# Gate and up of every second feed-forward tile as seven block products, on one Trainium2 core

## The chip, the cores and the metric

The kernel runs on one core of one Trainium2 chip. The time is device time in microseconds of one execution. Before the change it was 1366.73 us, the median of 3 runs (1365.81 to 1369.22).

## What is computed

The reference is a model of two layers on 512 tokens of width 1024, all in fp32. The first layer mixes tokens by two kinds of attention and then applies a feed-forward block; the second is a short convolution and a mixture of experts. The change touches the feed-forward block of the first layer alone, with a hidden width of 2816:

```
def swiglu(x, w_gate, w_up, w_down):
    return (jax.nn.silu(x @ w_gate) * (x @ w_up)) @ w_down

x = x + swiglu(rms_norm(x, ev_ffn_norm[i]), ffn_w_gate[i], ffn_w_up[i], ffn_w_down[i])
```

## The kernel before

**Precision.** An fp32 number is carried as two parts of type fp32r, "high" (a rounded copy, made on ScalarE) and "low" (the rest, a subtraction on VectorE); `split` (L517) makes such a pair. `mm3` (L512) makes one product of 128 rows in three matmuls: high times high, high times low, low times high. The sum is kept in PSUM.

**The feed-forward stage.** The hidden width is 22 tiles of 128 features (`NF`, index f). The normed input is held transposed in four buffers, `b0h`, `b0l`, `b1h`, `b1l` (each half of the model width, high and low, all 512 tokens). For one tile, `product_of_next` (L1404) takes one weight piece, runs `product` (L1383: 8 blocks of the model width, three matmuls of 512 columns each, so 24) into one PSUM bank, and releases the piece. It is called for gate and for up. `ff_tile` (L1411) then makes silu(gate) on ScalarE, the product with up on VectorE, and splits the result into hT[f] (ScalarE, then VectorE). `ff_down` (L1418) multiplies up to four finished tiles with the down weights: for each of 4 row blocks of 128 tokens and each half of the output columns it sums over the tiles in PSUM, and VectorE adds the sum into x. Within a row block the tiles are taken in order of f. The order is written out by `ffn_order` (L54): tiles 0 to 3, down for 0 and 1, tiles 4 to 7, down for 2 to 5, tiles 8 to 11, down for 6 to 9, and so on; tiles 20 and 21, down for 18 to 21. Tiles 0 and 1 are done together by `first` (L1387), in two halves of 256 tokens, while the norm of the last tokens is still being made.

**Weights.** `Weights` keeps a list of chunks (DMA loads of 512 KB) and of pieces (up to 128 x 1024 numbers, split into high and low). `pump` (L331) issues the next load when a raw buffer is free (on SyncE's queue), and otherwise the next split when its chunk is loaded and one of the part buffers is free: a copy on ScalarE (L351) and a subtraction on VectorE (L352). In this stage there are 6 raw buffers and 6 part buffers (`weight_room` "wa", L463, and "wb", L1270). `use` takes the next piece; `done` (L369) gives its part buffer back and pumps, so the split of the sixth piece on is written into the queues of ScalarE and VectorE at that place of the program:

```
def done(self, *pieces, splits=99):
    self.part_free += [p.slot for p in pieces]
    self.pump(splits)
```

**Order.** The program is scheduled by hand (`manual_schedule`): each engine works its instructions off in the order in which the code issues them; semaphores between engines are put in by the framework. PSUM is two pools of four banks: "p" (transposes, down products) and "g" (gate and up).

Of the kernel before, what the change touches and what calls it, by code (L numbers as in the profile page):

```python
# [13 lines left out]
F32 = mybir.dt.float32  # L14
F32R = mybir.dt.float32r
I32 = mybir.dt.int32
BF16 = mybir.dt.bfloat16
AF = mybir.ActivationFunctionType
OP = mybir.AluOpType
# [5 lines left out]
T = 512  # L25
D = 1024
NT = T // 128
KD = D // 128
# [6 lines left out]
NF = FF // 128  # L35
# [5 lines left out]
PACE = 2  # L41
GATE_UP_PACE = (1, 3, 2, 2)
NTINY = 8
MIX_ORDER = (1, 3, 0, "latent", "t0", "lq0", "c0", "lkv", "t1", "c1", "c2", "lq1", "k0", 2, "q", "k1")
WHOLE_HEADS = 2
WHOLE_TILES = 8
CW = 2048
PW = 1024
# [129 lines left out]
class Buf:  # L178


    def __init__(self, region, shape, dtype):
        self.region, self.shape, self.dtype = region, shape, dtype
        self.log, self.tile, self.before, self.over = [], None, None, False
        self.last, region.last = region.last, self
# [61 lines left out]
class Plan:  # L246
# [14 lines left out]
    def add(self, engine, n, issue, reads=(), writes=()):  # L261
        fixed, rate = self.RATE[engine]
        op = len(self.ops)
        deps = set()
        for bufs, write in ((reads, False), (writes, True)):
            for b in bufs:
                buf, part = b if isinstance(b, tuple) else (b, None)
                deps |= buf.touch(op, part, write)
        deps.discard(op)
        self.ops.append((engine, fixed + n / rate, issue, deps))  # L270
# [32 lines left out]
class Weights:  # L303
# [22 lines left out]
    def add_part(self, src, offset, row, at, k, n, keep=False):  # L326

        self.pieces.append(Piece(len(self.chunks), 0, k, n, keep))
        self.chunks.append((bass.AP(tensor=src.tensor, offset=src.offset + offset + at, ap=[[row, 128], [1, k * n]]), k * n))

    def pump(self, pieces=99):  # L331

        while True:
            if self.loaded < len(self.chunks) and self.raw_free:
                ap, m = self.chunks[self.loaded]
                pool, tag = slot = self.raw_free.pop(0)
                t = pool.tile([128, PW], F32, name=tag, tag=tag, bufs=1)
                self.nc.sync.dma_start(t[:, :m], ap)
                self.raw[self.loaded] = t, slot
                self.loaded += 1  # L340
            elif (pieces and self.ready < len(self.pieces) and self.pieces[self.ready].chunk in self.raw
                  and self.part_free):
                pieces -= 1
                p = self.pieces[self.ready]
                self.ready += 1
                raw, raw_slot = self.raw[p.chunk]
                pool, tag = p.slot = self.part_free.pop(0)
                p.t = pool.tile([128, 2, PW], F32R, name=tag, tag=tag, bufs=1)
                m = p.k * p.n
                src = raw[:, p.at:p.at + m]  # L350
                self.nc.scalar.copy(p.t[:, 0, :m], src)  # L351
                self.nc.vector.tensor_tensor(p.t[:, 1, :m], src, p.t[:, 0, :m].bitcast(F32), op=OP.subtract)  # L352
                if p.keep:
                    p.raw, p.raw_slot = self.raw.pop(p.chunk)
                else:
                    self.raw_free.append(self.raw.pop(p.chunk)[1])
            else:
                return
# [26 lines left out]

class Piece:
    def __init__(self, chunk, at, k, n, keep):
        self.chunk, self.at, self.k, self.n, self.keep = chunk, at, k, n, keep

    def hi(self, k, cols=slice(None)):  # L390
        return self.t[:, 0, k * self.n:(k + 1) * self.n][:, cols]
# [3 lines left out]

    def whole(self, k):
        return self.raw[:, k * self.n:(k + 1) * self.n]


class Act:  # L400
# [26 lines left out]
def kernel(ctx: ExitStack, tc: tile.TileContext, A, out, stop=None):  # L427
    nc = tc.nc
    PE, DVE, ACT, POOL = nc.tensor, nc.vector, nc.scalar, nc.gpsimd
# [26 lines left out]
    W = Weights(nc)  # L456
# [28 lines left out]
    og = od = 0  # L485
    for do, f in FFN_ORDER:
        if do == "up":
            og = W.add(A["w_gu"], og, (KD, 128), (KD, 128))
        else:
            for _ in range(0, f[1], 2):  # L490
                od = W.add(A["w_down"], od, (1, D), (1, D))
# [17 lines left out]
                off = W.add(A["w_ed"], off, (2, 512), (n - 2, 512), keep=True)  # L509


    def mm3(o, lh, ll, rh, rl, start, stop):  # L512
        PE.matmul(o, lh, rh, start=start, stop=False)  # L513
        PE.matmul(o, lh, rl, start=False, stop=False)  # L514
        PE.matmul(o, ll, rh, start=False, stop=stop)  # L515

    def split(hi, lo, src):  # L517
        ACT.copy(hi, src)  # L518
        DVE.tensor_tensor(lo, src, hi.bitcast(F32), op=OP.subtract)
# [60 lines left out]
    with ExitStack() as l0:  # L580
# [668 lines left out]
        for c in range(2):  # L1249
            ws = [take(), take()]  # L1250
            for i in range(NT):
                p = F2.buf([128, 512])
                s = slice(i * 128, (i + 1) * 128)
                for kb in range(2):
                    def go(p=p, s=s, kb=kb, w=ws[kb][0]):
                        for k in range(2):
                            mm3(p(), oh[0]()[:, 2 * kb + k, s], ol[0]()[:, 2 * kb + k, s], w.hi(k), w.lo(k),
                                kb == 0 and k == 0, kb == 1 and k == 1)
# [128 lines left out]
    def first(n, late, finish):  # L1387

        ws = []
        ps = [psB.tile([128, T], F32, name="pg", tag="g") for _ in range(n)]  # L1390
        for half in range(2):
            for j in range(n):
                if half == 0:
                    ws.append(W.use())
                product(ps[j], ws[j], slice(256 * half, 256 * half + 256))
                if half == 0 and j in late:
                    late[j]()
                if half == 1:
                    W.done(ws[j])
                    if j in finish:  # L1400
                        finish[j](ps)
        return ps

    def product_of_next():  # L1404
        w = W.use()
        p = psB.tile([128, T], F32, name="pg", tag="g")
        product(p, w, everything)
        W.done(w)
        return p

    def ff_tile(f, pg, pu):  # L1411
        sg = work.tile([128, T], F32, name="sg", bufs=2)
        hT[f] = work.tile([128, 2, T], F32R, name="hT", tag="hT", bufs=6)
        ACT.activation(sg, pg, AF.Silu)
        DVE.tensor_tensor(sg, pu, sg, op=OP.mult)
        split(hT[f][:, 0], hT[f][:, 1], sg)

    def ff_down(f0, nf, mid, end):  # L1418
# [18 lines left out]
        for f in range(nf):  # L1437
            del hT[f0 + f]

    nothing = lambda i: None  # L1440
    late = {0: lambda: transpose(2), 1: lambda: transpose(3)}
    for n, (do, f) in enumerate(FFN_ORDER):
        if do == "down":
            if n == len(FFN_ORDER) - 1:
                if stop == 2:
                    ff_down(*f, nothing, dump)
                    return
                xT2 = Act(act, "a")
                norm, transpose = normer(xT2, row_tile, psA, "p")
                ff_down(*f, *handover(norm, transpose))  # L1450
            else:
                ff_down(*f, nothing, nothing)
        elif f == 0:
            first(4, late, {1: lambda ps: ff_tile(0, *ps[:2]), 3: lambda ps: ff_tile(1, *ps[2:])})
        elif f > 1:
            pg = product_of_next()
            ff_tile(f, pg, product_of_next())
    load_gain(3)
    xT = xT2
# [6 lines left out]

    def conv_tile(j, pc, pu, pb):
        z = zs[j % 2]
        ct = work.tile([128, T], F32, name="sg", bufs=2)
        ACT.copy(ct, pc)  # L1470
        DVE.tensor_tensor(z[:, 2:], pu, ct, op=OP.mult)
        y = work.tile([128, T], F32, name="y", bufs=2)
        w = [pp[:, PP_CONV + 3 * j + a:PP_CONV + 3 * j + a + 1] for a in range(3)]
        DVE.tensor_scalar(y, z[:, 2:], w[2], None, op0=OP.mult)
        for a in (1, 0):
            DVE.scalar_tensor_tensor(y, z[:, a:a + T], w[a], y, op0=OP.mult, op1=OP.add)
        DVE.tensor_tensor(y, pb, y, op=OP.mult)
        split(yT.hi(j, everything), yT.lo(j, everything), y)
# [54 lines left out]
    def transpose(i):  # L1533

        hl = split_rows[i] = [work.tile([128, KD, 128], F32R, name="hT", tag="hT", bufs=6) for _ in range(2)]
        for b in range(2):
            pt = psA.tile([128, 4, 128], F32, name="pt", tag="p")
            for j in range(4):
                k = 4 * b + j
                PE.transpose(pt[:, j], xr[i][:, k * 128:(k + 1) * 128], ident)  # L1540
            split(hl[0][:, 4 * b:4 * b + 4], hl[1][:, 4 * b:4 * b + 4], pt)

    def logits(i):
        h, l = split_rows.pop(i)
        p = psB.tile([16, 128], F32, name="plT", tag="g")
        for k in range(KD):
            if k == 0:
                PE.matmul(p, wr[:, k], h[:, k], start=True, stop=False)
            PE.matmul(p[:8], wr[:, k, :8], l[:, k], start=False, stop=False)
            if k:  # L1550
                PE.matmul(p, wr[:, k], h[:, k], start=False, stop=k == KD - 1)
        lT = work.tile([16, 128], F32, name="sg", bufs=2)
        ACT.copy(lT, p)
        return lT

# [477 lines left out]
```

## Time and profile before

| | us |
|---|---|
| median of 3 runs | 1366.73 |
| the profiled execution | 1367.42 |
| its span | 1365.7 |
| TensorE busy | 1332.3 |
| VectorE busy | 844.6 |
| ScalarE busy | 688.8 |

Times in the profile are us from the span's start unless marked ns. PE is TensorE's matmul, PEld its weight load, DVE is VectorE, ACT ScalarE, POOL GpSimd, SP SyncE. PEclk is the granted TensorE clock as a share of 2.4 GHz. Matmuls are pipelined, so their bars overlap: the time between two starts is the pace, not the length of a bar. Names that begin with w, a, b or c and end in p, as `wap`, are part buffers of weights; `wbr` is a raw buffer.

### The profile page before, as it was taken

To read this page: it belongs to the slowest core of one execution; us is meant where nothing else is said; L and a number is where in the kernel's file an instruction comes from. 1 tells how busy PE (TensorE), PEld (TensorE's weight loads), DVE (VectorE), ACT (ScalarE), POOL (GpSimd) and SP (SyncE) were. 2 spreads that over 40 slices of the span, in tenths; PEclk is the share of its full clock that TensorE was granted. 3 is DMA by queue.
4 is the path that set the end of the run, shared out by engine and by line. 5 is a ranking of instruction groups with operands and counts; after the bars stand their busy time and mean duration, and the time that the engine had idled before them with its cause. 6 is when DMAs were issued, how large, how long until landed. Compare 5 with 4: busy or idle time off the path is not lost. (4 is left out here: it accounts for less than half of the span.)

```text
span 1365.7 us, 19159 instructions
## 1 busy us (share of the span) xinstructions
PE 1332.3 (98%) x6956; PEld 1061.4 (78%) x6957; DVE 844.6 (62%) x1365; ACT 688.8 (50%) x1144; POOL 208.2 (15%) x309
## 2 busy tenths in 40 slices
PE   7999899999999999999999999999999999999997
PEld 6866687879888888888898888888877878677774
DVE  4348897956433433434355444588888789786864
ACT  4535887854322222222242222377767678575763
POOL 2257554320000000000000000020111101201001
PEclk9999999999999999999999999999999999999999
DMA  5243101123321313132233222299997989979692
GB/s 191 88 157 113 32 17 47 47 101 124 116 93 63 131 61 133 62 124 75 95 109 108 93 93 78 103 340 321 401 341 258 358 326 399 324 250 338 231 342 53
DMA packets 69175, 229.83 MB, mean 168 GB/s; under 512 B 8768, under 2 KB 10060, under 8 KB 69068
## 3 DMA queue, kind: packets, MB, share of 16 engines
q1 hardware_dynamic: 64332, 217.39, 44.4%
q0 software_dynamic: 3392, 9.48, 2.9%
q10 hardware_dynamic: 1344, 1.58, 0.4%
q8 instruction: 62, 1.02, 0.3%
q14 instruction: 45, 0.37, 0.1%
HBM read 219.47 MB, written 8.94 MB: 167 GB/s over the span
## 5 line engine op out<-in xcount | busy, mean ns | idle before, releaser
L352 DVE TENSOR_TENSOR wbp<-wbr,wbp 128x1024 fp32r<-128x1024 f32 (+2 forms) x91 | 107.3, 1194 | 145.1 <-ACT wbp L351 143.2
L351 ACT CAST wbp<-wbr 128x1024 fp32r<-128x1024 f32 (+2 forms) x91 | 92.1, 1026 | 203.5 <-PE pg L515 109.1
L352 DVE TENSOR_TENSOR wap<-wbr,wap 128x1024 fp32r<-128x1024 f32 (+1 forms) x88 | 103.6, 1192 | 96.2 <-ACT wap L351 95.1
L351 ACT CAST wap<-wbr 128x1024 fp32r<-128x1024 f32 (+1 forms) x88 | 89.5, 1027 | 113.0 <-PE pg L515 73.5
L352 DVE TENSOR_TENSOR wap<-wcr,wap 128x1024 fp32r<-128x1024 f32 (+2 forms) x84 | 90.9, 1114 | 16.5 <-ACT wap L351 10.9
L352 DVE TENSOR_TENSOR wbp<-wcr,wbp 128x1024 fp32r<-128x1024 f32 (+2 forms) x83 | 91.6, 1129 | 12.4 <-ACT wbp L351 10.6
L524 POOL TENSOR_TENSOR rs<-rs,mhalf 128x1 f32<-128x1 f32 x11 | 6.1, 551 | 566.4 <-DVE rs L523 566.4
L351 ACT CAST wap<-wcr 128x1024 fp32r<-128x1024 f32 (+2 forms) x84 | 78.4, 962 | 18.7 <-DMA wcr<-w_eg 9.2
L351 ACT CAST wbp<-wcr 128x1024 fp32r<-128x1024 f32 (+2 forms) x83 | 79.4, 977 | 16.0 <-DMA wcr<-w_eg 6.5
L513 PE MATMUL pg<-wap,xgTh 128*128 128x512 f32 (+1 forms) x168 | 64.1, 382 | 0.7
L513 PE MATMUL pg<-wbp,xgTh 128*128 128x512 f32 (+1 forms) x162 | 61.7, 381 | 1.0
L515 PE MATMUL pg<-wap,xgTl 128*128 128x512 f32 (+1 forms) x168 | 62.5, 372 | 0.0
L514 PE MATMUL pg<-wap,xgTh 128*128 128x512 f32 (+1 forms) x168 | 62.4, 372 | 0.0
L514 PE MATMUL pg<-wbp,xgTh 128*128 128x512 f32 (+1 forms) x162 | 60.3, 372 | 0.0
L515 PE MATMUL pg<-wbp,xgTl 128*128 128x512 f32 (+1 forms) x162 | 60.3, 372 | 0.0
L1434 DVE TENSOR_TENSOR x<-pd,x 128x512 f32<-128x512 f32 x48 | 32.3, 689 | 39.2 <-PE pd L515 39.1
L612 POOL TENSOR_TENSOR s<-s,mhalf 128x4 f32<-128x4 f32 (+4 forms) x37 | 35.3, 963 | 70.2 <-DVE s L611 55.6
L1735 POOL DMA_INDIRECT xg<-xd,idx x15 | 22.9, 1530 | 140.6 <-DVE idx L1694 120.0
L636 DVE TENSOR_TENSOR wap<-r,wap 128x1024 fp32r<-128x1024 f32 (+3 forms) x24 | 26.2, 1091 | 26.5 <-ACT wap L633 26.4
L1897 POOL DMA_INDIRECT out_dram<-y,idx x7 | 14.9, 2128 | 174.5 <-ACT xe L1760 174.5
L513 PE MATMUL pd<-wap,hT 128*128 128x512 f32 x104 | 41.2, 396 | 0.0
L515 PE MATMUL pd<-wap,hT 128*128 128x512 f32 x104 | 41.1, 395 | 0.0
(531 smaller groups left out, 3926.4 us busy)
## 6 DMA issues: line engine op xcount, KB each, us to landing
wcr<-w_ed SPq DMA_DIRECT2D x50, 512.0 KB
wcr<-w_eg SPq DMA_DIRECT2D x45, 512.0 KB
wbr<-w_gu SPq DMA_DIRECT2D x44, 512.0 KB
wcr<-w_eu SPq DMA_DIRECT2D x40, 512.0 KB
wbr<-w_ed SPq DMA_DIRECT2D x30, 512.0 KB
wbr<-w_od_in SPq DMA_DIRECT2D x24, 512.0 KB
wbr<-w_eu SPq DMA_DIRECT2D x24, 512.0 KB
wbr<-w_down SPq DMA_DIRECT2D x22, 512.0 KB
```

Source lines behind the costliest of these rows:

```text
L351: self.nc.scalar.copy(p.t[:, 0, :m], src)
L352: self.nc.vector.tensor_tensor(p.t[:, 1, :m], src, p.t[:, 0, :m].bitcast(F32), op=OP.subtract)
L513: PE.matmul(o, lh, rh, start=start, stop=False)
L514: PE.matmul(o, lh, rl, start=False, stop=False)
L515: PE.matmul(o, ll, rh, start=False, stop=stop)
L524: POOL.tensor_tensor(dst, dst, mhalf[:p, :m], op=OP.pow)
L612: op("POOL", 70 + 78 * n, lambda: POOL.tensor_tensor(rs(), rs(), mhalf[:rs().shape[0], :n], op=OP.pow), (), [buf])
L636: op("DVE", m, lambda: DVE.tensor_tensor(p.t[:, 1, :m], src(), p.t[:, 0, :m].bitcast(F32), op=OP.subtract), [raw], [part])
L1434: DVE.tensor_tensor(x[i][:, cs], ps[c], x[i][:, cs], op=OP.add)
L1735: POOL.indirect_dma_start(out=t, out_offset=None, in_=src, in_offset=rows_of(e, b, n))
L1897: POOL.indirect_dma_start(out=out, out_offset=rows_of(e, 0), in_=y, in_offset=None, compute_op=OP.add)
```

## The change

Every odd tile from 3 to 21 (`SEVEN`, ten tiles) is computed as a product of 2 x 2 blocks: the two column blocks are gate and up, the model width is cut in two halves (the rows of the weights), and the tokens in two halves of 256. Seven products of blocks (each 4 blocks of 128 of the model width, three matmuls of 256 columns) take the place of eight. Sums of weight blocks are made on VectorE when a piece is split (four additions of 128 x 512; four pieces a tile in place of two, the last of them half as long, from the same 1 MB of weights). Sums of activation blocks are made once: POOL puts the high and low parts together again (`unsplit`), and VectorE and ScalarE make and split four sums after the gate product of tile 2 (`right_sums`). Four of the seven products are summed in one PSUM bank `a`, whose value is read between them; `b` and `e` are two halves of a second bank. ScalarE and VectorE collect the four results in `r`.

```
+SEVEN = tuple(range(3, NF, 2))
...
+    def add_products(self, src, offset, scratch):
+        for m in range(2):
+            self.chunks.append((bass.AP(tensor=src.tensor, offset=src.offset + offset + m * PW,
+                                        ap=[[2 * PW, 128], [1, PW]]), PW))
+        self.pieces += Products(self.nc, len(self.chunks) - 2, scratch).pieces
+        return offset + 128 * 2 * PW
...
+                if p.group:
+                    free = p.group.split(p, *(self.raw[p.group.chunk + j][0] for j in range(2)))
+                    if free is not None:
+                        self.raw_free.append(self.raw[free][1])
+                    continue
...
+class Products:
+    def __init__(self, nc, chunk, scratch):
+        self.nc, self.chunk, self.scratch = nc, chunk, scratch
+        self.pieces = [Piece(chunk + 1, 0, k, 128, False) for k in (8, 8, 8, 4)]
+        for p in self.pieces:
+            p.group = self
+
+    def split(self, p, a, b):
+        h, nc, j = PW // 2, self.nc, self.pieces.index(p)
+        add = nc.vector.tensor_tensor
+        if j == 0:
+            s = self.scratch()
+            self.src = [a, s, b, a[:, h:]]
+        src = self.src[j]
+        m = src.shape[1]
+        nc.scalar.copy(p.t[:, 0, :m], src)
+        if j == 0:
+            add(s[:, h:], a[:, :h], b[:, :h], op=OP.subtract)
+            add(b[:, :h], b[:, :h], b[:, h:], op=OP.add)
+            add(s[:, :h], b[:, :h], a[:, :h], op=OP.subtract)
+        add(p.t[:, 1, :m], src, p.t[:, 0, :m].bitcast(F32), op=OP.subtract)
+        if j == 0:
+            add(a[:, h:], a[:, h:], s[:, :h], op=OP.subtract)
+        return {2: self.chunk + 1, 3: self.chunk}.get(j)
...
-                og = W.add(A["w_gu"], og, (KD, 128), (KD, 128))
+            if f in SEVEN:
+                og = W.add_products(A["w_gu"], og, lambda: work.tile([128, PW], F32, name="sums", bufs=1))
+            else:
+                og = W.add(A["w_gu"], og, (KD, 128), (KD, 128))
...
-        sg = work.tile([128, T], F32, name="sg", bufs=2)
+        sg = work.tile([128, T], F32, name="sg", tag="R", bufs=2)
...
+    def unsplit(s):
+        for kb in range(2):
+            w = whole[kb, s] = work.tile([128, 4, T // 2], F32, name="whole", tag="hT", bufs=6)
+            POOL.tensor_tensor(w, xT.h[kb][:, :, tok2[s]].bitcast(F32), xT.l[kb][:, :, tok2[s]].bitcast(F32), op=OP.add)
+
+    def right_sums():
+        t1, t3, t4, t2 = whole[0, 0], whole[0, 1], whole[1, 0], whole[1, 1]
+        for dst, a, b in ((t1, t3, t1), (t3, t2, t3), (t2, t2, t1), (t4, t4, t2)):
+            DVE.tensor_tensor(dst, a, b, op=OP.subtract)
+        for j, t in ((2, t2), (3, t3), (1, t1), (4, t4)):
+            split(sums[j - 1][:, 0], sums[j - 1][:, 1], t)
...
+    def ff_products(f):
+        a, be = (psB.tile([128, 2, T // 2], F32, name="pg", tag="g") for _ in range(2))
+        a, b, e = a[:, 0], be[:, 0], be[:, 1]
+        r = work.tile([128, 3, T // 2], F32, name="R", bufs=2)
+        hT[f] = work.tile([128, 2, T], F32R, name="hT", tag="hT", bufs=6)
+
+        def go(p, w, k0, right, start):
+            for k in range(4):
+                mm3(p, w.hi(k0 + k), w.lo(k0 + k), right.hi(k), right.lo(k), start and k == 0, k == 3, more=not start)
+
+        def add(dst, x, y):
+            DVE.tensor_tensor(dst, x, y, op=OP.add)
+
+        w1 = W.use()
+        go(a, w1, 0, B11, True)
+        ACT.copy(r[:, 0], a)
+        go(b, w1, 4, B21, True)
+        W.done(w1)
+        w2 = W.use()
+        go(a, w2, 0, T2, False)
+        add(r[:, 0], b, r[:, 0])
+        ACT.copy(r[:, 1], a)
+        w3 = W.use()
+        go(e, w3, 0, T1, True)
+        ACT.copy(r[:, 2], e)
+        go(a, w2, 4, T3, False)
+        add(r[:, 2], a, r[:, 2])
+        W.done(w2)
+        w4 = W.use()
+        go(e, w4, 0, B22, False)
+        add(r[:, 1], e, r[:, 1])
+        ACT.activation(r[:, 0:2], r[:, 0:2], AF.Silu)
+        go(a, w3, 4, T4, False)
+        DVE.tensor_tensor(r[:, 0], a, r[:, 0], op=OP.mult)
+        DVE.tensor_tensor(r[:, 1], r[:, 2], r[:, 1], op=OP.mult)
+        two_of = lambda j: hT[f][:, j].rearrange("p (a t) -> p a t", a=2)
+        split(two_of(0), two_of(1), r[:, 0:2])
+        W.done(w4, w3)
...
+    unsplit(0)
+    late = {0: lambda: transpose(2), 1: lambda: transpose(3), 2: lambda: unsplit(1)}
...
+        elif f in SEVEN:
+            ff_products(f)
         elif f > 1:
             pg = product_of_next()
+            if f == 2:
+                right_sums()
             ff_tile(f, pg, product_of_next())
```

The buffers `ct` (convolution) and `lT` (router) also take the tag `R`, and `mm3` hands an argument for a check of open sums through.

## Rows read from the trace of the kernel before

**Rows 1.** The page: span, and busy time of the engines.
```profile
span 1365.7 us, 19159 instructions
PE 1332.3 (98%) x6956; PEld 1061.4 (78%) x6957; DVE 844.6 (62%) x1365; ACT 688.8 (50%) x1144; POOL 208.2 (15%) x309
```

**Rows 2.** Stretch: length; PE, PEld, DVE, ACT, POOL busy; clock, DMA share, GB/s.
```profile
321.00:612.00 291.00, 291.00 (x1361) 240.86 (x1360) 116.84 (x132) 81.97 (x98) 0.55 (x1) 1.00 0.31 103
```

**Rows 3.** Timeline, TensorE, from tile 3 on: start, length, line, out<-in, tile.
```profile
356.48 0.39 PE L513 MATMUL pg<-b0h,wbp 128*128 128x512 f32 x1
...
367.46 0.39 PE L513 MATMUL pd<-wap,hT 128*128 128x512 f32 x1
...
375.40 0.39 PE L514 MATMUL pd<-wap,hT 128*128 128x512 f32 x1
```

**Rows 4.** Timeline, TensorE, the 24 matmuls of 256 columns from 321.12.
```profile
321.12 0.28 PE L513 MATMUL pg<-b0h,wbp 128*128 128x256 f32 x1
...
323.83 0.28 PE L515 MATMUL pg<-b1h,wbp 128*128 128x256 f32 x1
...
321.36 0.19 PEld L513 LDWEIGHTS pg<-b0h,wbp 128*128 128x128 f32 x1
```

**Rows 5.** Timeline, ScalarE, end of tile 2's up product.
```profile
351.23 1.05 ACT L351 CAST wap<-wbr 128x1024 fp32r<-128x1024 f32 x1 [1.93 <-PE pg L515]
356.72 1.05 ACT L351 CAST wbp<-wbr 128x1024 fp32r<-128x1024 f32 x1 [4.44 <-PE pg L515]
357.67 0.59 ACT L1414 ACTIVATE sg<-pg 128x512 f32<-128x512 f32 x1
359.67 0.62 ACT L518 CAST hT<-sg 128x512 fp32r<-128x512 f32 x1 [1.40 <-DVE sg L1415]
```

**Rows 6.** Timeline, VectorE, the same place.
```profile
357.81 1.23 DVE L352 TENSOR_TENSOR wbp<-wbr,wbp 128x1024 fp32r<-128x1024 f32 x1 [4.27 <-ACT wbp L351]
358.95 0.68 DVE L1415 TENSOR_TENSOR sg<-pg,sg 128x512 f32<-128x512 f32 x1
360.32 0.69 DVE L519 TENSOR_TENSOR hT<-sg,hT 128x512 fp32r<-128x512 f32 x1 [0.69 <-ACT hT L518]
```

**Rows 7.** Timeline near 877: a ScalarE copy, and the matmul that waits for it.
```profile
876.16 1.05 ACT L518 CAST hT<-pt 128x512 fp32r<-128x512 f32 x2
877.10 0.25 ACT L1553 COPY sg<-plT 16x128 f32<-16x128 f32 x1
877.41 0.23 PE L1557 MATMUL pl<-ident,sg 16*128 16x16 f32 x1 [0.21 <-ACT sg L1553]
```

**Rows 8.** Groups by line and shape: count, busy us, mean ns.
```profile
L1760 ACT COPY xe<-pt 128x256 f32<-128x256 f32 x8 | 3.0, 370 | 0.0
L977 DVE TENSOR_TENSOR qm<-b,s 128x256 f32<-128x256 f32 x8 | 3.4, 421 | 2.6 <-POOL s L612 2.6
L1113 POOL TENSOR_TENSOR a1l<-v,a1h 128x512 fp32r<-128x512 f32 x4 | 5.1, 1286 | 9.3 <-ACT a1h L1112 9.3
```

**Rows 9.** Timeline, VectorE, the down product after tile 3.
```profile
371.86 2.48 DVE L1434 TENSOR_TENSOR x<-pd,x 128x512 f32<-128x512 f32 x4
```

**Rows 10.** Timeline, TensorE, after its idle time near 294.
```profile
294.57 0.47 PE L513 MATMUL po<-wap,a1h 128*128 128x512 f32 x1 [3.08 <-DVE x L1261]
294.87 0.40 PE L514 MATMUL po<-wap,a1h 128*128 128x512 f32 x1
...
295.86 0.63 PE L514 MATMUL po<-wap,a1h 128*128 128x512 f32 x1
296.29 0.63 PE L515 MATMUL po<-wap,a1l 128*128 128x512 f32 x1
```

**Rows 11.** Stretches of half a us: length, PE busy, granted clock, DMA share, GB/s.
```profile
295.50:296.00 0.50, 0.50 (x3) 0.50 0.00 0
...
298.00:298.50 0.50, 0.50 (x3) 0.50 1.01 352
298.50:299.00 0.50, 0.50 (x4) 0.87 1.09 270
```

More of the change, by code (lines that the diff above doesn't have):

```diff
@@ L387, in __init__ @@
     def __init__(self, chunk, at, k, n, keep):
-        self.chunk, self.at, self.k, self.n, self.keep = chunk, at, k, n, keep
+        self.chunk, self.at, self.k, self.n, self.keep, self.group = chunk, at, k, n, keep, None
     def hi(self, k, cols=slice(None)):
@@ L509, with mm3 @@
                 off = W.add(A["w_ed"], off, (2, 512), (n - 2, 512), keep=True)
[L512 to L515, printed above, removed]
+    def mm3(o, lh, ll, rh, rl, start, stop, more=False):
+        for x, y, first, last in ((lh, rh, start, False), (lh, rl, False, False), (ll, rh, False, stop)):
+            PE.matmul(o, x, y, start=first, stop=last, skip_group_check=more)
     def split(hi, lo, src):
@@ L1438, in ff_down, with __init__ @@
             del hT[f0 + f]
+    sums = [act.tile([128, 2, 4, T // 2], F32R, name=f"t{j + 1}", tag=t, bufs=1)
+            for j, t in enumerate(("a0h", "a0l", "a1h", "a1l"))]
+    tok2 = [slice(0, T // 2), slice(T // 2, T)]
+    class Half:
+        def __init__(self, kb, s):
+            self.hi = lambda k: xT.hi(4 * kb + k, tok2[s])
+            self.lo = lambda k: xT.lo(4 * kb + k, tok2[s])
+    class Sum:
+        def __init__(self, j):
+            self.hi = lambda k: sums[j - 1][:, 0, k]
+            self.lo = lambda k: sums[j - 1][:, 1, k]
@@ new lines @@
+    whole = {}
+    def unsplit(s):
[8 more added lines that the diff above has]
+            split(sums[j - 1][:, 0], sums[j - 1][:, 1], t)
@@ new lines @@
+    B11, B21, B22, T1, T2, T3, T4 = Half(0, 0), Half(1, 0), Half(1, 1), Sum(1), Sum(2), Sum(3), Sum(4)
+    def ff_products(f):
[33 more added lines that the diff above has]
+        W.done(w4, w3)
@@ L1440 @@
     nothing = lambda i: None
-    late = {0: lambda: transpose(2), 1: lambda: transpose(3)}
+    unsplit(0)
+    late = {0: lambda: transpose(2), 1: lambda: transpose(3), 2: lambda: unsplit(1)}
     for n, (do, f) in enumerate(FFN_ORDER):
@@ L1468, in conv_tile @@
         z = zs[j % 2]
-        ct = work.tile([128, T], F32, name="sg", bufs=2)
+        ct = work.tile([128, T], F32, name="ct", tag="R", bufs=2)
         ACT.copy(ct, pc)
@@ L1551, in logits @@
                 PE.matmul(p, wr[:, k], h[:, k], start=False, stop=k == KD - 1)
-        lT = work.tile([16, 128], F32, name="sg", bufs=2)
+        lT = work.tile([16, 128], F32, name="lT", tag="R", bufs=2)
         ACT.copy(lT, p)
```

## The prediction

> **What bounds the kernel now.** I read the page's busy shares first: TensorE is busy 98% of the span, VectorE 62%, ScalarE 50% [rows 1]. Then the table by stretches: the change lies in the feed-forward stage, 321 to 612 us, and there TensorE is busy in all of its 291 us while VectorE works 117 and ScalarE 82 [rows 2]. So the stage is as long as its matmuls, and any new TensorE wait is paid in full. Then TensorE in order of time: gate and up of one tile are 48 matmuls of 512 columns, the first at 356.48, the first after them at 367.46 [rows 3], so 10.98 us, 0.229 each. Matmuls of 256 columns exist already at the start of the stage: 24 from 321.12, the last at 323.83 [rows 4], so 0.1178 each. Bars overlap in these rows; starts, not durations, give the pace. Last, ScalarE and VectorE around the end of an up product [rows 5, 6], since their queues run in written order, and the new products stand behind that order.
>
> A profiled execution took 1367.42 us against a span of 1365.7; the median of the runs is 1366.73. What follows is a difference on the profiled one, added to the median.
>
> **The matmuls.** Ten tiles (3, 5, ... 21) go from 48 matmuls of 512 columns to 7 products of 12 with 256: 84 x 0.1178 = 9.90 us for 10.98. Ten times, that is -10.9 us, and all there is to win. Per product 1.41 us. Each matmul has its own weight load of 0.19 us that starts while another runs [rows 4], and the pace stays at 0.118, so loads are hidden. The Trainium skill, "TensorE: Matmul & The Clock Gate", section "The mechanism" of its part on packing, says that a load overlaps a running matmul only where the row group differs; with its P/1.2 for 128 columns, about 107 ns (an estimate), 36 more loads a tile would make ten tiles 38 us worse. The trace's pace disagrees, and I go by it.
>
> **First new wait: the third product waits for a copy.** The seven products go a, b, a, e, a, e, a. The third adds onto `a`, which ScalarE must have copied to `r` before. That copy stands in ScalarE's queue behind the work on the even tile before. Counted from the odd tile's first matmul (356.48): split of the piece that the up product's release starts, 0.24 to 1.29 on ScalarE, then 1.33 to 2.56 on VectorE; VectorE's product with silu from 2.47; ScalarE's hT copy from 3.19, VectorE's second half of hT from 3.84 [rows 5, 6]. The new copy follows the hT copy after 0.52 (two 512-element copies in a row take 1.05 [rows 7]), at 3.71, and takes 0.37 [rows 8]: 4.08. TensorE follows ScalarE by 0.06 [rows 7]: 4.14. The two products of cover end at 2.83. **Stall 1.31 us**, more than the 1.09 that a tile wins. Nine tiles: +11.8.
>
> In tile 3 the four activation sums stand in front as well. Released by tile 2's gate product (at 350.99, 0.24 before ScalarE's 351.23 [rows 5]), VectorE does the piece's split to 353.5, four subtractions of 1024 elements at 1.15 a piece (the pace of the splits) to 358.1, four halves to 362.7, then the split of the up product's piece, the product with silu (363.9), and only then ScalarE's hT copy and the copy of `a`: 365.5. The third product was due at 356.48 + 2.83 = 359.3. **+6.2 once.** What POOL adds (four sums of 1024 elements, by its 1.29 for 512 [rows 8] 2.6 each, 10.3 in all) begins near 324 and is wanted after 353, so it costs nothing.
>
> **Second new wait: the fourth product waits for VectorE.** `b` and `e` are halves of one [128, 2, 256] tile, one PSUM bank. I take it that the framework orders a matmul into a bank behind an earlier read of it by another engine, though in other columns. No row shows such a case. If so, `e` waits until VectorE has added `b` to `r`. That add stands behind the split of the piece that the release of w1 starts. Six part buffers mean that it is the sixth piece on. In tiles 3, 7, 11, 15, 19 and 21 that is a plain one: VectorE is free at 4.45, the split starts when ScalarE has cast, at 5.07, takes 1.14, the add 0.42 [rows 8], and TensorE starts at 6.75, the third product having ended at 5.55: 1.2 us, six times, +7.2. In tiles 5, 9, 13 and 17 the sixth piece is the first of the next odd tile, which carries four more operations of 512 elements at about 0.6 (four in 2.48 us [rows 9]) and their dependences: VectorE is free of it at 8.2, TensorE starts at 8.67: 3.1 us, four times, +12.4. Bounds: 0 if the halves are tracked apart, +19.6 if not. I take +19.6, as the buffer is allocated as one bank. Here the Trainium skill, "PSUM — Partial Sum Buffer", section "PSUM bank collisions raise a hardware error", has a rule: guard PSUM by bank and quadrant, not by address. No run here shows it; it is on the side of the higher end, and the other end is a rival below.
>
> The other reads are covered: the copies of `a` and `e` and the add into r[2] each have one product of 1.41 us over them and need 0.24 + 0.37 (0.42) + 0.1. Silu and hT end some 2.9 us after the tile; the down product asks for that tile last, 4.2 us in (18 matmuls at 0.233; 34 of them take 7.94 [rows 3]).
>
> **Third: the down product after tile 3.** Tile 3's last release starts the splits of tile 5's first two pieces; on VectorE they stand before the adds into x. Two feature tiles make 2.8 us a row block (12 matmuls), four PSUM buffers serve two blocks, so block 2 waits for block 0's adds. VectorE is some 7.6 us behind there, and they are due at 5.6: **+2.8 once.** Before, these adds came 4.4 us after the product's first matmul [rows 3, 9].
>
> **The clock.** At 291.5 TensorE stood idle 3.08 us for a VectorE add; 0.8 us after its return the granted clock fell to 0.50, the 1.2 GHz level, until 298.5, and matmuls came every 0.43 instead of 0.233 [rows 10, 11]. Eight such, 1.55 us lost. Five stalls here are at least as long (tile 3 and four of 3.1). I charge four falls, +6.0, as tile 3's partly runs inside its second wait; bounds 0 and ten falls, +15.
>
> **At nothing.** Weight bytes and loads are the same. Each odd tile holds its two raw buffers longer, but they are loaded a tile ahead and the DMA engines are busy 0.31 of the stage [rows 2]. VectorE gains some 5.5 us a tile, 55 on 117 of 291, ScalarE about half that: neither becomes the bound; they cost through queue order. Tag changes for `sg`, `ct` and `lT` move nothing, and later stages are unchanged.
>
> Sum: -10.9 + 11.8 + 6.2 + 19.6 + 2.8 + 6.0 = +35.5 us; 1366.7 + 35.5 = **1402**. Without clock falls 1396, with ten 1411.
>
> **Rivals.** (1) The halves of the bank are tracked apart: the second wait goes (-19.6) and with it four of the five long stalls: -10.9 + 11.8 + 6.2 + 2.8 + 1.5 = +11.4, 1378. For it: the columns are disjoint. Against: one tile, one bank. (2) Faster: the partial sums are read while products cover them. It decides on ScalarE's queue: the copy of `a` has to end 1.31 us sooner, before 2.83, and the same must hold for the sums in tile 3 and for `e`. Then -10.9 is left plus 2.8: 1359. For it: without a piece split at the up product's release the chain would be 2.2 us shorter. Against: such a split stands at the end of every up product [rows 5]. (3) The change doesn't do what it says: the 256-column products run slower in this order. At 0.131 a matmul (10.98 / 84) the gain is nil; for it, a restart after a stall costs 0.07 more [rows 10], and each switch could; against, 24 in a row at 0.118 [rows 4]. With the waits 1413.
>
> **Chances.** Forecast 0.73, rival 1 0.12, rival 2 0.07, rival 3 with a clock that falls oftener 0.08. A measurement of this kernel can tell about 0.3%, 4 us. Rival 2 in part (only some stalls there) may land within it, so faster 0.05, same 0.04, slower 0.91. The range takes in rival 1 and the ten falls: 1378 to 1413.
>
> **What would show it.** In the changed profile: matmuls of odd tiles 0.118 apart; TensorE idle before the third product on ScalarE's copy into R, 1.3 us, and 6 in tile 3; idle before the fourth on VectorE's add, 1.2 and 3.1 in the pattern named; a granted clock of 0.5 in slices of the stage. I am wrong if the stage isn't longer than 291 us, if there is no idle before the fourth product, or if the time is lost elsewhere than on TensorE.

## The result, and the profile after

The changed kernel takes 1404.93 us (median of 4 runs, 1404.37 to 1405.9) against 1367.45 for the kernel before on the same chip: a ratio of 1.0275, with a 95% interval of 1.0263 to 1.0288. It is slower by 37.5 us, where +35.5 was forecast. The profiled execution took 1405.22 us; the page gives its span and busy shares, which answer to [rows 1]:

```profile
span 1403.2 us, 20099 instructions
PE 1331.4 (95%) x7316; PEld 1075.6 (77%) x7317; DVE 916.6 (65%) x1473; ACT 718.2 (51%) x1198; POOL 220.2 (16%) x313
```

TensorE has 360 matmuls more (ten tiles, 84 for 48) and is busy as long as before, but the span has 37.5 us more. The feed-forward stage begins and ends at landmarks that both traces show: the first gate matmul of 256 columns, and the first matmul of the convolution's products, which reads `a0h`. Before, these stand at 321.12 [rows 4] and at:

```profile
692.36 0.28 PE L513 MATMUL pg<-a0h,wbp 128*128 128x256 f32 x1
```

In the timeline of the changed kernel:

```profile
319.83 0.28 PE L563 MATMUL pg<-b0h,wbp 128*128 128x256 f32 x1
...
728.39 0.28 PE L563 MATMUL pg<-a0h,wap 128*128 128x256 f32 x1
```

So the stage takes 408.56 us for 371.24, and its 37.3 us more are nearly the whole of the span's growth (37.5). (The stretch of [rows 2] is a part of this stage.) By stretches, in the columns of [rows 2], first the kernel before and then the changed one:

```profile
321.00:692.00 371.00, 371.00 (x1713) 305.57 (x1712) 152.12 (x176) 105.47 (x129) 2.19 (x4) 1.00 0.29 96
```
```profile
320.00:728.00 408.00, 370.25 (x2071) 320.41 (x2071) 224.57 (x283) 134.49 (x183) 13.59 (x8) 0.98 0.26 87
```

TensorE was never idle; now it is idle for 37.75 us, and its clock stands at 0.98. VectorE works 55% of the stage, ScalarE 33%: neither is the bound. The waits of TensorE by releaser (us in total, times, longest), of which these four lines are the stage's and add up to all of its idle time, say who it waits for:

```profile
PE pg L563 <- ACT R L1537: 16.6, 10, 6.3
PE pg L563 <- DVE R L1533: 16.4, 9, 3.0
PE pd L563 <- DVE x L1482: 2.8, 1, 2.8
PE pg L563 <- DVE wap L366: 1.9, 1, 1.9
```

The first is ScalarE's copy of `a` (before the third product), the second VectorE's add of `b` (before the fourth), the third the down product after tile 3. The fourth was not forecast. TensorE's rows in tiles 3, 5 and 7 (start, length, and in brackets the idle time and who ended it):

```profile
368.29 2.93 PE L563 MATMUL pg<-t,wbp 128*128 128x256 f32 x12 [6.31 <-ACT R L1537]
...
385.65 2.93 PE L563 MATMUL pd<-wap,hT 128*128 128x512 f32 x6 [2.84 <-DVE x L1482]
...
408.11 1.68 PE L563 MATMUL pg<-t,wap 128*128 128x256 f32 x12 [1.10 <-ACT R L1537]
412.82 4.61 PE L563 MATMUL pg<-t,wap 128*128 128x256 f32 x24 [3.03 <-DVE R L1533]
...
435.18 1.68 PE L563 MATMUL pg<-t,wap 128*128 128x256 f32 x12 [1.21 <-ACT R L1537]
437.72 1.69 PE L563 MATMUL pg<-t,wbp 128*128 128x256 f32 x12 [0.86 <-DVE R L1533]
```

A bracket counts from the end of the bar before, and a bar of 0.28 ends 0.16 after its turn of 0.118 is over; so from start to start the waits are 0.16 longer: 1.26 and 3.19 us in tile 5, 1.37 and 1.02 in tile 7. Tiles 9, 13 and 17 repeat tile 5; tiles 11, 15, 19 and 21 repeat tile 7. Why they come is seen in the queues of ScalarE and VectorE behind tile 5's first matmul (404.03):

```profile
405.18 0.59 ACT L1462 ACTIVATE sg<-pg 128x512 f32<-128x512 f32 x1
407.17 0.62 ACT L566 CAST hT<-sg 128x512 fp32r<-128x512 f32 x1 [1.40 <-DVE sg L1463]
407.70 0.36 ACT L1537 COPY R<-pg 128x256 f32<-128x256 f32 x1
...
409.83 0.37 ACT L1543 COPY R<-pg 128x256 f32<-128x256 f32 x1 [0.82 <-PE pg L563]
```
```profile
407.82 0.69 DVE L567 TENSOR_TENSOR hT<-sg,hT 128x512 fp32r<-128x512 f32 x1 [0.68 <-ACT hT L566]
408.43 0.69 DVE L436 TENSOR_TENSOR sums<-wbr,wbr 128x512 f32<-128x512 f32 x1
...
411.74 0.69 DVE L441 TENSOR_TENSOR wbr<-wbr,sums 128x512 f32<-128x512 f32 x1
412.35 0.42 DVE L1533 TENSOR_TENSOR R<-pg,R 128x256 f32<-128x256 f32 x1
```

The copy of `a` (L1537) stands behind the even tile's split of hT; the add (L1533) behind the five operations by which the next odd tile's first piece is made, though its operand `b` was complete long before.

The granted clock, by stretches (columns as in [rows 2]):

```profile
331.00:334.00 3.00, 3.00 (x16) 3.00 (x16) 3.00 (x5) 0.00 (x0) 1.40 (x1) 0.50 0.94 269
...
365.00:371.50 6.50, 3.21 (x15) 3.21 (x16) 4.57 (x6) 2.22 (x5) 0.00 (x0) 0.50 0.26 84
...
385.50:388.50 3.00, 2.85 (x7) 2.28 (x8) 1.89 (x4) 0.00 (x0) 0.00 (x0) 0.50 0.02 5
413.00:416.00 3.00, 3.00 (x15) 3.00 (x16) 0.00 (x0) 0.21 (x1) 0.00 (x0) 0.50 0.00 0
417.00:648.00 231.00, 212.41 (x1175) 182.32 (x1174) 115.67 (x154) 72.69 (x98) 0.00 (x0) 1.00 0.26 89
```

Four stretches are at 0.50, the 1.2 GHz level, each behind a wait. Behind tile 5 there are none up to 648, though the 3.03 us wait comes three times more.

### The profile page after: what moved, and what is told of

Its sections match the earlier page's. It is cut to its first block, busy times and chain, and to the rows that moved or that the text cites. A ratio compares the mean times of both kernels' runs of the same rounds, so it can differ in the third digit from the quotient of the medians.

```text
span 1403.2 us, 20099 instructions
## 1 busy us (share of the span) xinstructions
PE 1331.4 (95%) x7316; PEld 1075.6 (77%) x7317; DVE 916.6 (65%) x1473; ACT 718.2 (51%) x1198; POOL 220.2 (16%) x313
## 5 line engine op out<-in xcount | busy, mean ns | idle before, releaser
L366 DVE TENSOR_TENSOR wbp<-wbr,wbp 128x1024 fp32r<-128x1024 f32 (+1 forms) x81 | 97.7, 1220 | 88.6 <-ACT wbp L365 84.4
L366 DVE TENSOR_TENSOR wap<-wbr,wap 128x1024 fp32r<-128x1024 f32 (+2 forms) x78 | 95.3, 1235 | 75.5 <-ACT wap L365 75.4
L365 ACT CAST wbp<-wbr 128x1024 fp32r<-128x1024 f32 (+1 forms) x81 | 82.3, 1026 | 103.5 <-PE pg L563 68.7
L365 ACT CAST wap<-wbr 128x1024 fp32r<-128x1024 f32 (+2 forms) x78 | 78.4, 1019 | 80.4 <-PE pg L563 53.3
L366 DVE TENSOR_TENSOR wap<-wcr,wap 128x1024 fp32r<-128x1024 f32 (+2 forms) x83 | 92.4, 1125 | 18.7 <-ACT wap L365 14.6
L366 DVE TENSOR_TENSOR wbp<-wcr,wbp 128x1024 fp32r<-128x1024 f32 (+2 forms) x84 | 91.1, 1116 | 10.5 <-ACT wbp L365 8.6
L563 PEld LDWEIGHTS pg<-wbp,xgTh 128*128 128x128 f32 x332 | 60.3, 188 | 15.5 <-issue 5.1
L563 PE MATMUL pd<-wbp,hT 128*128 128x512 f32 x288 | 71.8, 396 | 0.0
L563 PEld LDWEIGHTS pg<-wap,xgTh 128*128 128x128 f32 x328 | 59.5, 188 | 14.4 <-issue 5.5
L563 PEld LDWEIGHTS pd<-wbp,hT 128*128 128x128 f32 x288 | 53.9, 188 | 13.1
L563 PE MATMUL b<-wap,a0h 128*128 128x512 f32 (+2 forms) x192 | 56.8, 381 | 0.0
L1482 DVE TENSOR_TENSOR x<-pd,x 128x512 f32<-128x512 f32 x48 | 31.8, 686 | 36.0 <-PE pd L563 35.9
L563 PE MATMUL pg<-b1h,wbp 128*128 128x256 f32 (+1 forms) x192 | 50.8, 337 | 0.0
## 6 DMA issues: line engine op xcount, KB each, us to landing
wbr<-w_eu SPq DMA_DIRECT2D x24, 512.0 KB, 10.9
```

The source lines that it names most:

```text
L563: PE.matmul(o, x, y, start=first, stop=last, skip_group_check=more)
L1482: DVE.tensor_tensor(x[i][:, cs], ps[c], x[i][:, cs], op=OP.add)
```

## The experiments

All are edits of the changed kernel; each compared with the kernel before, which stood at 1366.95 to 1367.77 us on the same chip.

**A bank of its own for `e`.**

```
-        a, be = (psB.tile([128, 2, T // 2], F32, name="pg", tag="g") for _ in range(2))
-        a, b, e = a[:, 0], be[:, 0], be[:, 1]
+        a, b = (psB.tile([128, 2, T // 2], F32, name="pg", tag="g")[:, 0] for _ in range(2))
+        e = psA.tile([128, 2, T // 2], F32, name="pe", tag="p")[:, 0]
```

> The two products e get a PSUM bank of their own (from the pool of the transposes) instead of the other half of b's bank. Theory (the fourth product waits for VectorE's add of b only because b and e share a bank): the gaps before the fourth product, 1.0 to 1.1 us in tiles 7, 11, 15, 19, 21 and 3.2 in tiles 5, 9, 13, 17, vanish, and with them the clock fall of tile 5: about -18.6 - 1.5, so 1385 us (1382 to 1388). Rival (the columns are tracked apart, the wait is for something else of VectorE): unchanged, 1405.

Measured: 1384.43 us (ratio 1.0118, 1.0102 to 1.0133), 20.5 less than the changed kernel. In tile 5 the third product still waits, and the fourth (now into `pe`) follows it without a gap:

```profile
409.86 1.68 PE L563 MATMUL pg<-t,wap 128*128 128x256 f32 x12 [1.10 <-ACT R L1537]
411.38 1.57 PE L563 MATMUL pe<-t,wap 128*128 128x256 f32 x12
```

The wait comes from the sharing: 17.9 us of waits are gone, and with the wait in tile 5 the fall of the clock behind it. (The fall at 331 is gone too, though the 1.9 us wait ahead of it is still there; the last section comes back to that.) This edit gives `e` another tile and another bank at once, so it does not say which of the two the framework goes by. In SBUF it keeps the parts of one tile apart: in the changed kernel ScalarE's second copy into `r` (L1543, at 409.83) runs before VectorE's add into another part of it (L1533, at 412.35), which was issued first. The result agrees with the rule of the Trainium skill that the prediction weighed ("PSUM — Partial Sum Buffer", section "PSUM bank collisions raise a hardware error"): the program guards the whole bank, or the tile that fills it, and not the columns. It does not show what the chip would do without the guard.

**The same wait, with the bank left shared.** The release of w1 starts a weight split ahead of the add; here the split comes later.

```
         go(b, w1, 4, B21, True)
-        W.done(w1)
+        W.done(w1, splits=0)
```

> Edit to the changed kernel: the weight tile that the second product frees is not split at once, but after the next one is taken up, so that this split's VectorE and ScalarE work stands behind the first of the two sums; b and e still share one bank, all else as in the changed kernel. Theory (the fourth product waits for VectorE's sum of b, which is late chiefly because of the split queued ahead of it): the wait shrinks to about the cost of the sum alone less the 4.6 us of the third product that cover it, so to nothing in nearly all of the nine tiles; the time is about that of the version with banks of their own, 1383 to 1388 us, less or more what a weight that is ready later may cost. Rival (the shared bank itself orders the two, whatever the queue holds): the gaps of 1.1 and 3.3 us stay and so does 1405 us.

Measured: 1386.08 us (1.0129, 1.0113 to 1.0144). The add now follows hT directly:

```profile
408.93 0.69 DVE L567 TENSOR_TENSOR hT<-sg,hT 128x512 fp32r<-128x512 f32 x1 [0.68 <-ACT hT L566]
409.54 0.42 DVE L1533 TENSOR_TENSOR R<-pg,R 128x256 f32<-128x256 f32 x1
```

Sharing makes the fourth product ask for the add, and the split ahead of the add makes the answer late. Undoing either half of the pair takes most of that loss away (20.5 us above, 18.9 here), with all the work still done.

**The even tile's work behind the copy of `a`.**

```
-    def ff_products(f):
+    def ff_products(f, even):
...
-        hT[f] = work.tile([128, 2, T], F32R, name="hT", tag="hT", bufs=6)
...
         ACT.copy(r[:, 0], a)
+        ff_tile(f - 1, *even)
+        hT[f] = work.tile([128, 2, T], F32R, name="hT", tag="hT", bufs=6)
         go(b, w1, 4, B21, True)
...
-            ff_products(f)
+            ff_products(f, even)
...
-            ff_tile(f, pg, product_of_next())
+            even = pg, product_of_next()
```

> The even tile's silu, product and split are issued after the odd tile's first copy of a, so that the copy is ahead of them in ScalarE's queue; b and e still share a bank. Theory (VectorE's queue sets when the add of b is done, and that doesn't move): the gap before the third product goes, the one before the fourth grows by as much, and the time stays, 1405, up to 1409 if the longer single gaps make the clock fall in more tiles. Rival (the two waits add up independently): nine tiles of 1.3 us less, 1393.

Measured: 1419.36 us (1411.83 to 1419.51; 1.0358, 1.0334 to 1.0381), worse than every case that was priced. The waits themselves went as the theory has it: they moved from the third to the fourth product, with nearly the same total.

```profile
PE pg L563 <- DVE R L1532: 31.8, 10, 4.6
PE pg L563 <- ACT R L1536: 3.0, 1, 3.0
```

To take away the first of two waits on one chain took nothing off their sum: 34.8 us here, 33.0 in the changed kernel. What nobody priced is the clock. The view of the cores (span, mean granted clock), first of the changed kernel, then of this one:

```profile
core 0: 1403.2 us, clock 0.989
```
```profile
core 0: 1417.3 us, clock 0.976
```

At 0.989 of 1403.2 us, 15.4 us of full speed are missing; at 0.976 of 1417.3, 34.0. The difference, 18.6, is more than the 14.4 by which this kernel is slower (a part of it falls into time in which TensorE waits anyway). The clock stood at 0.50 in ten stretches of the stage instead of four: two up to tile 3, four behind the longer single waits (4.5 to 4.6 us by the brackets in tiles 5, 9, 13 and 17), and four behind waits of 2.1 to 2.2 us in tiles 11, 15, 19 and 21, while the same wait in tile 7 has none.

**Both edits together:** the bank of its own, and the even tile's work behind the copy.

> Both edits at once: e in its own bank, and the copy of a issued ahead of the even tile's work. Theory (two waits by queue order, and nothing else, between the saved matmuls and the measured time): tiles 5 to 21 take about 10.0 us each instead of 14.6 and 12.4, tile 3's gap falls from 6.4 to about 3: 1370 us (1366 to 1374). Rival (the 256-column products are slower in this order than in the stage's first products): tiles of 11 us and more, 1380 or above.

Measured: 1371.09 us (1.0025, 1.0015 to 1.0036). What is left waits here:

```profile
PE pg L563 <- DVE R L1532: 3.2, 4, 0.9
PE pg L563 <- ACT R L1536: 3.1, 1, 3.1
PE pd L563 <- DVE x L1482: 2.8, 1, 2.8
PE pg L563 <- DVE wap L366: 1.9, 1, 1.9
```

The two waits of the odd tiles, with the falls of the clock behind them, are most of the loss: without them 33.8 of the 37.5 us are back. The new first line is the last product of tiles 5, 9, 13 and 17, which adds onto `a` and asks for VectorE's add into r[:, 2], behind the same heavy weight split.

**GpSimd's sums (unforeseen wait), first try.** `unsplit(0)` was issued later, ahead of `unsplit(1)`.

```
-    unsplit(0)
-    late = {0: lambda: transpose(2), 1: lambda: transpose(3), 2: lambda: unsplit(1)}
+    late = {0: lambda: transpose(2), 1: lambda: transpose(3), 2: lambda: (unsplit(0), unsplit(1))}
```

> The first two of POOL's four sums (the high and low parts put together again) are issued later, after the transposes of the last tokens, and nothing else is changed. Theory (VectorE's instructions take twice as long and more while POOL adds 128x1024 numbers, which made TensorE wait 2.1 us near 328 us for a weight split, and a clock fall of 1.5 us followed): that gap goes, -3.6 us, 1401. Rival (the gap is due to a later load or to ScalarE): unchanged, 1405.

Measured: 1408.68 us (1.0305, 1.0291 to 1.0319), and the edit moved nothing: GpSimd's queue holds nothing between the two places and `unsplit(0)` waits for nothing later, so its sums started in the same place and the 1.91 us wait stayed. The experiment tells nothing of the theory. It tells something of the measurement: in the traces every engine runs the same instructions in the same order as in the changed kernel, and yet this one took 3.7 us more, and the two intervals do not touch. Its clock stood at 0.50 for 23.9 us of the stage instead of 17.1, in part behind waits of 3.0 us in tiles 13 and 17 that have no fall in the trace of the changed kernel. So a difference of this size between two versions can come from the clock alone.

**Second try:** behind `unsplit(1)`, which waits for the last transposes.

```
-    unsplit(0)
-    late = {..., 2: lambda: unsplit(1)}
+    late = {..., 2: lambda: (unsplit(1), unsplit(0))}
```

> Edit to the changed kernel: GpSimd's two sums over the first half of the tokens are issued behind its two over the second half, which wait for the last transposes of the normed rows; nothing else. Theory (GpSimd's 128x1024 sums and VectorE's work on the same rows slow each other: the norm row of 3.41 us and the weight split of 2.26 us each, where the kernel before has 1.28 and 1.18): with the sums out of 322.8 to 328.5, VectorE's rows there go back to about 1.3 and 1.2 us, the matmul of line 563 at about 330 no longer waits 1.91 us for the weight split, and the fall of the clock behind it (half speed for 3.41 us) goes too or moves. The time falls by 2 to 4 us, to 1401 to 1403 us. Rival (VectorE is late for a reason of its own, such as the order of its queue): the 1.9 us wait stays and the time is 1405 us.

Measured: 1404.28 us (1400.87 to 1405.98; 1.0266, 1.0252 to 1.0281). The wait and the fall behind it went, but the median missed its band, and the time is not told apart from that of the changed kernel: two of the five runs lie near 1401 with a mean clock of 0.990, three at 1404 to 1406 with 0.986 to 0.987. The trace tells more. VectorE and GpSimd in the changed kernel:

```profile
322.88 3.41 DVE L605 SCALAR_TENSOR_TENSOR xn<-x,rs,gain 128x1024 f32<-128x1024 f32 x1 [0.73 <-POOL rs L572]
326.21 4.52 DVE L366 TENSOR_TENSOR wap<-wbr,wap 128x1024 fp32r<-128x1024 f32 x2
...
322.81 2.40 POOL L1508 TENSOR_TENSOR whole<-b0h,b0l 128x1024 f32<-128x1024 f32 x1
325.16 3.34 POOL L1508 TENSOR_TENSOR whole<-b1h,b1l 128x1024 f32<-128x1024 f32 x1
...
329.64 0.51 PE L563 MATMUL pg<-b0h,wap 128*128 128x256 f32 x2 [1.91 <-DVE wap L366]
```

And in this one, where GpSimd comes later:

```profile
322.89 1.29 DVE L605 SCALAR_TENSOR_TENSOR xn<-x,rs,gain 128x1024 f32<-128x1024 f32 x1 [0.73 <-POOL rs L572]
324.10 2.36 DVE L366 TENSOR_TENSOR wap<-wbr,wap 128x1024 fp32r<-128x1024 f32 x2
...
335.18 2.90 DVE L436 TENSOR_TENSOR sums<-wbr,wbr 128x512 f32<-128x512 f32 x1
338.12 2.78 DVE L437 TENSOR_TENSOR wbr<-wbr 128x512 f32<-128x512 f32 x1
...
334.14 3.40 POOL L1508 TENSOR_TENSOR whole<-b0h,b0l 128x1024 f32<-128x1024 f32 x1
337.50 2.85 POOL L1508 TENSOR_TENSOR whole<-b1h,b1l 128x1024 f32<-128x1024 f32 x1
```

The norm row takes 1.29 us alone and 3.41 beside GpSimd; additions and subtractions of 512 elements, 0.69 alone (L436 in the queue of VectorE above), take 2.90 and 2.78 beside it. The bars show turns, not sharing: the norm row that began 0.07 us after GpSimd's sum ends about one length of its own after that sum's end (322.81 + 2.40 + 1.29 = 326.5; it ended at 326.29), and GpSimd's next sum, queued behind it in turn, shows 3.34 for 2.40. The Trainium skill has this as a rule ("SBUF — State Buffer", section "Who interferes with whom"): a VectorE instruction with two inputs in SBUF and a GpSimd instruction that reads SBUF use one read port in turns, the later one blocked for the whole of the other. These rows agree with it.

**The same move where fewer waits disturb the reading,** as one more edit on the version with both.

> Edit to the version with banks of its own for the second and the fourth product and the even tile's work behind the first copy (1371.1 us): GpSimd's first two sums are issued behind its last two; nothing else. With fewer waits the clock falls in fewer places, so that the sums' price can be read in the time. Theory: the 1.91 us wait at about 329 and the fall of the clock behind it go: 1366.5 to 1369 us. Rival (the wait comes back as another at the next place, since VectorE has no time to spare there): 1371 us, with a new wait before 360 us.

Measured: 1368.38 us (1366.55 to 1369.62; 1.0006, 0.9997 to 1.0015), 2.7 us below that version (the two intervals just touch), and the line of `wap L366` is gone from the waits. By time alone that could be the clock, as the first try showed; the place says more. From the stage's first matmul to the first of tile 3 that version takes 39.2 us and this one 36.0 (the kernel before 35.4). So GpSimd's sums cost some 3 us there, the fall behind the wait included, though GpSimd had nobody waiting for it.

**The sums over the tokens, earlier.**

```
-            pg = product_of_next()
             if f == 2:
                 right_sums()
+            pg = product_of_next()
```

> Edit to the changed kernel: the sums over the tokens are issued ahead of the second tile's gate product instead of behind it, 5.5 us of TensorE's work earlier; nothing else. Theory (tile 3's long wait is only the queue of VectorE behind these sums): the 6.6 us gap before tile 3's third product shrinks to the 1.3 to 1.5 of the other odd tiles, so the time falls by some 5 us, and by 1.7 to 3.4 us more if the clock no longer falls there: 1397 to 1400 us. Rival (VectorE then carries the backlog along, because its work in this part is more than TensorE's): the gap stays above 3 us and the time is 1402 us or more.

Measured: 1404.3 us (1.0267, 1.0252 to 1.0283). The rival holds. VectorE's work was moved, not taken away, and it carries it along: four subtractions and four halves without a pause, then two weight splits (in the rows left out), and only then the even tile's product.

```profile
350.05 5.07 DVE L1514 TENSOR_TENSOR whole<-whole 128x1024 f32<-128x1024 f32 x4
355.03 4.62 DVE L567 TENSOR_TENSOR t<-whole,t 128x1024 fp32r<-128x1024 f32 x4
...
361.85 0.68 DVE L1463 TENSOR_TENSOR sg<-pg,sg 128x512 f32<-128x512 f32 x1
```

The gap before the third product fell from 6.59 us only to 4.02 (start to start), the fourth's came back (1.14), and the clock stayed down for 6.8 us instead of 3.4 at the down product and fell in tile 9 too. The time did not move.

**The down product's adds ahead of the weight splits.**

```
-        W.done(w4, w3)
+        W.done(w4, w3, splits=0 if f == 3 else 99)
```

> Edit to the changed kernel: after tile 3 alone, the weight splits that its last release starts are held back, so that they stand behind the down product's adds; nothing else. Theory (the down product's 2.8 us wait is those two splits ahead of its adds): the wait of line 563 for VectorE's x goes, the clock's fall of 3.41 us behind it goes too, and the time falls by 2.8 to 4.5 us, to 1400 to 1402 us. Rival (VectorE is so far behind tile 3's own sums that the adds are late anyway): a wait of over 1 us stays there and the time is within 1 us of 1405.

Measured: 1403.1 us (1401.61 to 1404.86; 1.0265, 1.0249 to 1.028). The wait for `x L1482` and the fall behind it are gone from the trace (span 1399.6), so the cause is as predicted. But the median missed its band: in this trace the clock stood at 0.50 from 481 to 484, in tile 9, where the changed kernel's kept full speed behind the same wait of 3.0 us. By time alone the interval does not tell it from the changed kernel.

**Everything at once:** the bank and the copy, GpSimd's second try, the sums, the down product, and the split of w1 behind the add.

> Edit to the changed kernel: everything that a wait was found for at once: banks of their own for the second and the fourth product; the even tile's activation, product and split issued behind the copy of the first product; the split of the freed weight tile behind the first sum; the sums over the tokens ahead of the second tile's gate product; GpSimd's first sums behind its last; the weight splits behind tile 3 held back so that they stand behind the sums of the down product. Theory: all the waits that the change added are gone, the odd tiles run at 84 x 0.118 = 9.9 us against 11.0 before, and the nine tiles give some 9 x 1.1 = 10 us: 1357 to 1361 us, faster than before. Rival (the version with the bank and the copy alone, 1371 us, is bounded by the total work of VectorE and ScalarE, so that a wait taken away comes back at the next place): 1367 to 1371 us.

Measured: 1357.47 us (1356.06 to 1358.36), ratio 0.9922, 0.9909 to 0.9936: faster than the kernel before by 10.1 us. By stretches, from the stage's first matmul to its last, and the waits of TensorE in it:

```profile
321.00:681.00 360.00, 357.23 (x2074) 312.83 (x2073) 223.66 (x284) 134.63 (x183) 14.13 (x8) 1.00 0.29 100
```
```profile
PE pg L563 <- ACT R L1536: 1.9, 1, 1.9
PE pg L563 <- ACT R L1544: 0.5, 1, 0.5
```

All the work of the change is still there (VectorE 223.66 us for 224.57), and the stage takes some 360 us for 371. The rival, that VectorE and ScalarE bound it, falls. Tile 3 still waits, 1.9 and 0.5 us, and tile 2 0.4 us for ScalarE. Against the version at 1368.4 us the traces place the 10.9 us that came on top: 2.0 in tile 3, 4.7 in the down product after it, 0.8 to 1.2 in each of tiles 5, 9, 13 and 17. The edits behind these were not run one by one on that version.

## Why the prediction was right

The sign, the mechanism and the size held: 1404.9 in a range of 1378 to 1413. By its steps, in the trace of the changed kernel:

- **The matmuls** (-10.9): 84 starts 0.118 apart where nothing waits, so 9.9 us a tile. The working took 10.98 us for every tile before; five of the ten took 11.2, so the gain is 11.9. Nothing is seen of the 38 us that more weight loads were to cost by the rule that the prediction set aside. With the waits out, the stage is 11.3 us shorter than before.
- **First wait** (+11.8): 1.25 to 1.37 in nine tiles, 11.7 in all. The chain came as worked out: copy at 3.67 us after the tile's first matmul (3.71 predicted), third product at 4.08 (4.14). **Tile 3** (+6.2): 6.47.
- **Second wait** (+19.6): 3.19 for 3.1 in four tiles, 1.02 for 1.2 in five, and about 0.1 for 1.2 in tile 3, where the third product comes so late that the add is done. Together 17.9. The assumption on the bank, which no row of before showed, held: the first experiment takes the sharing away and the wait with it; the second shows the other half, the split ahead of the add.
- **Down product after tile 3** (+2.8): 2.84 by the bracket, 3.0 from start to start. VectorE came to these adds 7.9 us after the product's first matmul (7.6 predicted). The two numbers in the working, 7.6 and 5.6, give 2.0; 2.8 needs the add itself, 0.7 us, which the working does not name.
- **The clock** (+6.0): the size is about right, the places are not, so the size is luck. The four stretches at 0.50 last 17.1 us; TensorE was busy in 13.6 of them, so they cost 6.8. Four falls were charged for five stalls, tile 3's and the four of 3.1 us. Four there were, but only two behind such a stall (tile 3 and tile 5); the others stood behind the wait of the down product and one of 1.9 us. The step took [rows 10, 11] as a rule that a long wait brings a fall, and the runs don't bear that out. (The fall in those rows began at 295.2, 0.65 us after TensorE's return and not 0.8; its cost is hardly touched by that.)
- **"At nothing": GpSimd's sums.** This step failed. It asked whether anybody waits for GpSimd's result, and nobody did; it did not ask what VectorE's instructions cost beside it. They became 2 to 3 times as long, and TensorE waited 1.9 us (2.07 from start to start) for a weight split, with a fall of the clock behind it (1.7 us of speed lost). The first part of the stage grew by 3.8 us, a tenth of the whole loss.
- **The restarts** were named, not charged: the two products behind a wait ran at 0.127 a matmul, about 0.2 us a tile, some 1.9 in ten.

The sum of what was measured: -11.9 + 11.7 + 6.5 + 17.9 + 3.0 + 6.8 + 2.1 + 1.9 = +38.0, against 37.3 in the stage. What had no place in the forecast's sum (GpSimd 2.1, the restarts 1.9) and what came out larger (the clock by 0.8, tile 3 and the down product by 0.5) was half made good by the second wait (1.7 less) and the gain (1.0 more). That the total came within 2 us is thus in part luck; the terms that carry it, the two waits and tile 3, each came within 2 us by themselves.

Rival 1 (no wait from the bank) is refuted by the waits for L1533. Rival 2's price, 1359, was right for a kernel that it said did not exist: with the queue orders changed it is 1357.5. It let ScalarE's queue decide, and that was too little: the copy ahead, without a way out for the fourth product, made things worse. Rival 3's slow matmuls did not come.

## What to carry to other kernels

A product that is summed in PSUM and read in between makes TensorE wait for two other engines' queues, so ask of each read what stands ahead of it in written order: weight splits that stood ahead of a sum cost some 18 us here by their place alone, as long as two results shared a bank. Price waits on one chain together: the first of the two, taken away alone, came back at the next product and brought more falls of the clock, while the second could go by itself. And "off the critical path" is not yet "at nothing": an engine that no one waits for can still lengthen another's instructions.

## What the runs showed of the hardware

VectorE and GpSimd, both adding from SBUF, took turns: 0.69 us became 2.90 and 2.78 (second try of GpSimd's sums), and 1.29 became 3.41 (changed kernel).

The length of a wait did not decide whether the granted clock fell behind it. The wait of 1.9 us near 329 stands in eight of the traces (the changed kernel and seven edits), and in three of them the clock fell behind it. The wait of 3.0 us in tiles 5, 9, 13 and 17 stands in five traces, twenty times in all, and in nine cases the clock fell. Times of one kernel spread where such waits are: 1400.87 to 1405.98 us in the second try of GpSimd's sums, where the two fastest runs are those with the highest mean clock; 1356.06 to 1358.36 with everything at once, where hardly any wait is left and the trace has no fall in the stage. What decides a single fall stays open.
